# Five modulation slices summed along the rows by VectorE, and a norm turned by plain transposes, in a two-layer trunk kernel

## The chip, the cores and the metric

One core of a Trainium2 chip runs the whole kernel. Time is device microseconds, from the start of the program to its end; the median of 3 runs counts. The engines are named PE (TensorE), DVE (VectorE), ACT (ScalarE), POOL (GpSimd) and SP (SyncE, which here only issues loads).

## The reference

256 tokens of 1024 values pass two layers. A layer is a token mixer and a channel mixer; each stands behind an RMS norm, and a vector c modulates the norm's result and the residual:

```python
c_act = jax.nn.silu(c)
for layer in range(DEPTH):
    mod = c_act @ ada_w[layer] + ada_b[layer]
    sh_m, sc_m, gt_m, sh_f, sc_f, gt_f = [m[:, None, :] for m in jnp.split(mod, 6, axis=-1)]
    h = modulate(rms_norm(x, norm_mix_g[layer]), sh_m, sc_m)      # h * (1 + sc) + sh
    x = x + gt_m * hybrid_mixer(h, ...)
    h = modulate(rms_norm(x, norm_ffn_g[layer]), sh_f, sc_f)
    f = swiglu(h, ...) if layer % 2 == 0 else moe_swiglu(h, ...)
    x = x + gt_f * f
return rms_norm(x, final_g)
```

The mixer is a matrix product to 3088 columns, a gated recurrence and chunked linear attention, and an output projection. Layer 0's channel mixer is a dense SwiGLU (1024 to 2816), layer 1's picks 2 of 8 experts of that size per token. Everything is float32. What matters here is `mod`: for each layer six slices of 1024 values, each a product of one row of 1024 with a 1024 x 1024 matrix (4 MB of weights a slice, 48 MB in all).

## The kernel before, in words

**Weights.** Every weight comes from device memory in units of 128 x 2048 values (1 MB). `load` (L131 to 134) takes one of six buffers `raw` and issues the load on SP, whose queue runs in order; a buffer is free once all who read its last content are done. For most products `split` (L137 to 147) makes of 128 x 1024 weights a rounded part `whi` (ACT, L145) and the rest `wlo` (DVE, L146), in five buffers each; a product is then three matmuls, high x high, high x low and low x high (`mm3`, L155 to 159, or `stationary_pair`, L406 to 408, where the weights are the stationary operand).

**Modulation.** `ada` (L237 to 303) makes one slice in four steps, one unit of weights each, and a last step that finishes it. It has two ways. On PE (`on_dve` false): per unit four matmuls (eight records in the trace), whose stationary operand is silu(c) spread over 32 columns, add up into a bank `pb` (L261). On DVE: per unit two multiply-adds of 128 x 1024 into `acc` (L266; the first is a TENSOR_SCALAR, L264), and at the end ones-matmuls (L286) add `acc` over the partitions. For shifts and scales both ways end alike: ACT copies the bank to a `row` (L289), PE turns it by four transposes (L226) so that the values lie along partitions, and DVE adds the bias (L297, L299) and, for a scale, makes (1 + sc) * g (L301). A gate ends as a row on all partitions (L271 to 279). `put` queues slices, and `fill(n)` lets the next n steps be written at that place (L306 to 331). Which way a slice goes stands in the table `ON`: on PE sh_m, sc_m, gt_m, sh_f of layer 0 and sh_m, sc_m, gt_f of layer 1; on DVE sc_f and gt_f of layer 0 and gt_m, sh_f, sc_f of layer 1.

**Norm.** `residual` (L411 to 443) ends a layer's half: for each half of the tokens t and half of the columns c DVE multiplies the product by the gate (`y`, L440) and adds it to the stream `xs` (L441); then `block(t, c)` squares on ACT (L338). After c = 1, `rms` makes 1/rms per token (DVE L344, POOL L345), DVE scales the identity by it (`dg`, 128 x 128, L360), and PE multiplies the tokens by that diagonal (L364, eight products a half), which scales and turns them in one go. When both halves are there, ACT applies shift and scale (`h`, L377), and DVE makes of it `wide_hi` and `wide_lo` (L380, L381) for the next products. `hold` (L384) puts the first splits behind parts of that. Layer 1's last norm (`block` of the router) goes another way and isn't touched.

**Order.** The program is written in the order of the driver (L1295 to 1320): the first norm, mixer 0, dense layer (its first four fill steps, `AT_DENSE`, stand ahead of its first product), mixer 1, experts. A scheduler then sets each engine's own order from a time line that it estimates when the program is built; on the chip each engine runs its queue strictly in that order, and waits at an instruction whose operands aren't there.

Of the kernel before, what the change touches and what calls it, by code (L numbers as in the profile page):

```python
# [61 lines left out]
def trunk(  # L62
# [174 lines left out]
    def ada(layer, kind, on_dve=True, bank=pb):  # L237

        n = ("sh_m", "sc_m", "gt_m", "sh_f", "sc_f", "gt_f").index(kind)
# [11 lines left out]
        if not on_dve:  # L251
            ps = bank()
        for j in range(4):
            w = load(ada_w[layer, n, j])
# [25 lines left out]
        else:  # L280
            r = P
            if on_dve:
                r = 64
                ps = pm()
                for h in range(2):
                    pe.matmul(ps[32 * h:32 * h + 32, :], ones[:, 0:32], acc[:, h * 512:(h + 1) * 512],  # L286
                              start=True, stop=True)
# [1109 lines left out]
```

## Time and profile before

| what | value |
|---|---|
| median of 3 runs | 1167.55 us (1165.86 to 1170.02) |
| the profiled execution | 1168.7 us, its span 1166.9 us |
| granted PE clock, mean | 0.979 |
| PE busy | 1107.4 us (95%) |
| DVE busy | 627.4 us (54%) |
| ACT busy | 518.3 us (44%) |
| DMA | 395.69 MB, mean 339 GB/s |

The span is first to last instruction of one profiled execution; its own time is a little longer, and it lies 1.15 us above the median. The stages in it: first norm to about 37 us, mixer 0 to about 149, norm and dense layer to about 356, norm and mixer 1 to about 467, router and experts to the end. A granted clock of 1.00 is 2.4 GHz, 0.50 is 1.2 GHz. A busy PE counts matmuls whose ends are modelled, so 95% doesn't say that PE runs at its peak.

### The profile page before, as it was taken

To read this page: it belongs to the slowest core of one execution; us is meant where nothing else is said; L and a number is where in the kernel's file an instruction comes from. 1 tells how busy PE (TensorE), PEld (TensorE's weight loads), DVE (VectorE), ACT (ScalarE), POOL (GpSimd) and SP (SyncE) were. 2 spreads that over 40 slices of the span, in tenths; PEclk is the share of its full clock that TensorE was granted. 3 is DMA by queue.
4 is the path that set the end of the run, shared out by engine and by line. 5 is a ranking of instruction groups with operands and counts; after the bars stand their busy time and mean duration, and the time that the engine had idled before them with its cause. 6 is when DMAs were issued, how large, how long until landed. Compare 5 with 4: busy or idle time off the path is not lost.

```text
span 1166.9 us, 15801 instructions
## 1 busy us (share of the span) xinstructions
PE 1107.4 (95%) x6125; PEld 742.8 (64%) x6125; DVE 627.4 (54%) x818; ACT 518.3 (44%) x724; POOL 30.5 (3%) x69
## 2 busy tenths in 40 slices
PE   4899999999999999899999999999999999998993
PEld 2578779999777888686465445554455544655540
DVE  2668556757776765797135443353343633345442
ACT  2764444444437744786234333542342333434331
POOL 2000000000001000300000000000000000000000
PEclk9899999999999999899999999999999999998996
DMA  9977486858886447495999999999999999999994
GB/s 361 410 288 291 145 324 249 310 201 306 334 332 229 147 143 288 181 359 189 418 420 419 420 419 420 419 420 420 388 406 419 420 419 419 419 419 403 398 420 172
DMA packets 57182, 395.69 MB, mean 339 GB/s; under 512 B 8294, under 2 KB 8710, under 8 KB 9356
## 3 DMA queue, kind: packets, MB, share of 16 engines
q1 hardware_dynamic: 54272, 393.24, 84.2%
q10 hardware_dynamic: 2828, 1.37, 0.4%
q8 instruction: 50, 0.82, 0.3%
q14 instruction: 32, 0.26, 0.1%
HBM read 393.53 MB, written 1.05 MB: 338 GB/s over the span
## 4 chain that ended last, share of the span: by engine, by line
PE 88%; DMA 4%; ACT 3%; DVE 2%; POOL 1%; issue 1%; ACTq 0%; POOLq 0%; DVEq 0%; SPq 0%
PE pa L1050 17%; PE pa L158 8%; PE pa L157 8%; PE pa L159 8%; PE po L1099 7%; PE pa L406 6%; PE pa L407 6%; PE pa L408 6%; PE pb L158 4%; PE pb L159 4%; PE pb L157 4%; PE pm L226 2%; PE pb L261 2%; PE pm L973 2%; DMA bdx<-in_wx_dram 2%; ACT whi L145 2%
## 5 line engine op out<-in xcount | busy, mean ns | idle before, releaser
L146 DVE TENSOR_TENSOR wlo<-raw,whi 128x1024 fp32r<-128x1024 f32 x318 | 378.6, 1222 | 205.1 <-ACT whi L145 204.4
L145 ACT ACTIVATE whi<-raw 128x1024 fp32r<-128x1024 f32 x318 | 324.5, 1057 | 214.7 <-PE pa L407 90.2
L1050 PE MATMUL pa<-raw,x_n 128*64 128x512 f32 (+3 forms) x960 | 205.0, 562 | 0.0
L406 PE MATMUL pa<-wide_hi,whi 128*128 128x256 f32 x544 | 154.3, 284 | 0.2 <-DVE wide_hi L380 0.2
L407 PE MATMUL pa<-wide_lo,whi 128*128 128x256 f32 x544 | 153.5, 282 | 0.2 <-DVE wide_lo L381 0.2
L408 PE MATMUL pa<-wide_hi,wlo 128*128 128x256 f32 x544 | 153.5, 282 | 0.0
L1050 PEld LDWEIGHTS pa<-raw,x_n 128*64 128x64 f32 (+1 forms) x960 | 63.0, 131 | 106.7 <-issue 101.3
L158 PE MATMUL pa<-wlo,x_hi 128*128 128x512 f32 (+1 forms) x288 | 113.3, 394 | 3.7 <-DVE wlo L146 3.7
L157 PE MATMUL pa<-whi,x_hi 128*128 128x512 f32 (+1 forms) x288 | 110.7, 389 | 0.9 <-ACT whi L145 0.3
L159 PE MATMUL pa<-whi,x_lo 128*128 128x512 f32 (+1 forms) x288 | 109.9, 382 | 0.1
L406 PEld LDWEIGHTS pa<-wide_hi,whi 128*128 128x128 f32 x544 | 102.3, 188 | 6.4 <-issue 4.0
L407 PEld LDWEIGHTS pa<-wide_lo,whi 128*128 128x128 f32 x544 | 102.5, 189 | 1.6 <-issue 1.1
L408 PEld LDWEIGHTS pa<-wide_hi,wlo 128*128 128x128 f32 x544 | 102.5, 188 | 0.3 <-issue 0.3
L1099 PE MATMUL po<-raw,big 128*64 128x512 f32 (+1 forms) x440 | 93.4, 616 | 6.3 <-DMA raw<-in_m_dram 6.3
L1053 ACT ACTIVATE s<-pa 128x512 f32<-128x512 f32 (+1 forms) x30 | 16.9, 562 | 163.4 <-PE pa L1050 163.4
L158 PE MATMUL pb<-wlo,a_hi 128*128 128x512 f32 x176 | 71.6, 408 | 2.0 <-DVE wlo L146 2.0
L158 PEld LDWEIGHTS pa<-wlo,x_hi 128*128 128x128 f32 x288 | 55.3, 192 | 26.5 <-DVE wlo L146 6.7
L159 PE MATMUL pb<-whi,a_lo 128*128 128x512 f32 x176 | 69.8, 398 | 0.0
L157 PEld LDWEIGHTS pa<-whi,x_hi 128*128 128x128 f32 x288 | 55.3, 192 | 21.8 <-issue 7.7
L157 PE MATMUL pb<-whi,a_hi 128*128 128x512 f32 x176 | 60.8, 403 | 2.0 <-ACT whi L145 2.0
L1099 PEld LDWEIGHTS po<-raw,big 128*64 128x64 f32 (+1 forms) x440 | 25.4, 132 | 57.8 <-issue 49.8
L159 PEld LDWEIGHTS pa<-whi,x_lo 128*128 128x128 f32 x288 | 55.5, 193 | 10.0 <-DVE x_lo L986 0.8
(323 smaller groups left out, 1242.4 us busy)
## 6 DMA issues: line engine op xcount, KB each, us to landing
raw<-in_m_dram SPq DMA_DIRECT2D x263, 1024.0 KB, 10.6
raw<-in_ada_w_dram SPq DMA_DIRECT2D x48, 1024.0 KB, 7.3
raw<-in_f_dram SPq DMA_DIRECT2D x33, 1024.0 KB, 6.0
raw<-in_win_dram SPq DMA_DIRECT2D x20, 1024.0 KB, 6.3
raw<-in_wout_dram SPq DMA_DIRECT2D x8, 1024.0 KB, 6.1
xs<-in_x_dram SPq DMA_DIRECT2D x1, 1024.0 KB
big<-in_m_dram SPq DMA_DIRECT2D x1, 1024.0 KB
out_dram<-big SPq DMA_DIRECT2D x2, 512.0 KB, 3.2
```

The lines of the kernel that those rows point to most:

```text
L145: act.activation(hi[:, :n], src, AF.Copy)
L146: dve.tensor_tensor(lo[:, :n], src, hi[:, :n].bitcast(F32), op=ALU.subtract)
L157: pe.matmul(ps, l_hi, r_hi, start=first, stop=False)
L158: pe.matmul(ps, l_hi, r_lo, start=False, stop=False)
L159: return pe.matmul(ps, l_lo, r_hi, start=False, stop=last)
L226: return pe.transpose(o, i, ident[:i.shape[0], :i.shape[0]])
L261: pe.matmul(ps[o:o + 32, :], cact[:, k, :], wi[:, h * 512:(h + 1) * 512], start=(j == 0), stop=(j == 3))
L406: pe.matmul(pv[:, b, :], wh, h_hi[:, k, :], start=(k == 0), stop=False)
L407: pe.matmul(pv[:, b, :], wh, h_lo[:, k, :], start=False, stop=False)
L408: pe.matmul(pv[:, b, :], wl, h_hi[:, k, :], start=False, stop=(k == KD - 1))
L1050: pe.matmul(ps[r:r + m, :n], x_n[:, k, :], w[:, kk * n:(kk + 1) * n], start=(k < js), stop=(k >= KD - js))
L1099: pe.matmul(acc[r:r + m, :], aa["a_n"][:, k, :], w[:, i * 1024 + c * 512:i * 1024 + (c + 1) * 512], start=(k < js), stop=(k >= KF - js))
```

## The change

Five slices (layer 0's sc_f; layer 1's sh_m, sc_m, sh_f, sc_f) are made in a third way. Their weights lie transposed in memory: a partition holds an output value's 1024 weights. DVE multiplies them by a row silu(c) that lies on all partitions (`crow`, loaded at the start by a broadcast of 0.5 MB and passed through Silu on ACT), and one instruction's accumulator output gives the finished sum of 128 output values (`accum_out`); two such sums a unit, eight a slice, then DVE adds the bias and for a scale multiplies by g. PE and ACT have no part in it. The two gates that DVE summed stay as they were; all others stay on PE.

In the norm `dg` and the product by it go. DVE scales the tokens themselves (`tn`, 128 x 512, two a half, two buffers), and PE turns them by plain transposes, eight a half. In the first norm of all, the first split is held behind the last instruction of sc_m's modulation.

```diff
+KINDS = ("sh_m", "sc_m", "gt_m", "sh_f", "sc_f", "gt_f")
+
+SUMMED = ((0, "sc_f"), (1, "sh_m"), (1, "sc_m"), (1, "sh_f"), (1, "sc_f"))
...
+    crow = const([P, D], F32, "crow", pre)
+    act.dma_start(crow[:], c_row.to_broadcast([P, D]))
+    act.activation(crow[:], crow[:], AF.Silu)
+
+    def ada_summed(layer, kind):
+
+        n = KINDS.index(kind)
+        m = cst.tile([P, KD], F32, tag=f"{kind}{layer}", name=f"{kind}{layer}")
+        for j in range(4):
+            w = load(ada_w[layer, n, j])
+            for i in range(2):
+                b = 2 * j + i
+                acc = pre.tile([P, D], F32, tag="acc", name=nm("acc"))
+                dve.scalar_tensor_tensor(acc[:], w[:, i * D:(i + 1) * D], 1.0, crow[:], op0=ALU.mult, op1=ALU.mult,
+                                         accum_out=m[:, b:b + 1])
+            yield
+        dve.tensor_tensor(m[:], m[:], col("ab", 48 * layer + 8 * n, KD), op=ALU.add)
+        if kind[:2] == "sc":
+            dve.scalar_tensor_tensor(m[:], m[:], 1.0, col("nmg" if kind == "sc_m" else "nfg", 8 * layer, 8),
+                                     op0=ALU.add, op1=ALU.mult)
+        mod[kind, layer] = m
+        yield
+
+    def ada(layer, kind):
+        if (layer, kind) in SUMMED:
+            return ada_summed(layer, kind)
+        return ada_across(layer, kind, (layer, kind) in ((0, "gt_f"), (1, "gt_m")))
...
             rs = rms(t)
-            dg = pre.tile([P, P], F32, tag=f"dg{t}", name=nm("dg"))
-            dve.tensor_scalar(dg[:], ident[:], rs[:], 32.0, op0=ALU.mult, op1=ALU.mult)
             if t == 0:
                 turned.extend(b() for b in ((pa,) * 4 if alone else BANKS))
-            for k in range(KD):
-                pe.matmul(turned[k // 2][:, (k % 2) * SEQ + t * P:(k % 2) * SEQ + (t + 1) * P],
-                          xs[:, t, k * P:(k + 1) * P], dg[:], start=True, stop=True)
+            for j in range(2):
+                tn = pre.tile([P, 4, P], F32, tag="tn", name=nm("tn"), bufs=2)
+                dve.tensor_scalar(tn[:], xs[:, t, j * 512:(j + 1) * 512], rs[:], 32.0, op0=ALU.mult, op1=ALU.mult)
+                for i in range(4):
+                    k = 4 * j + i
+                    transpose(turned[k // 2][:, (k % 2) * SEQ + t * P:(k % 2) * SEQ + (t + 1) * P], tn[:, i, :])
...
-            hold((n0,), *((n, *m) for n, m in zip(ns, marks)))
+            hold((n0, *modded) if alone else (n0,), *((n, *m) for n, m in zip(ns, marks)))
```

The scheduler's order changes with it at two places. The first is DVE at the end of layer 0's output projection, up to the norm ahead of the dense layer. Before (`y` and `xs` of the second half of the tokens, `rs`, `dg`; the three `wlo` belong to the dense layer):

```order
L360 TENSOR_SCALAR dg_1258<-ident,rs_1255 128x128
L441 TENSOR_TENSOR xs<-xs,y_1284 128x512
L146 TENSOR_TENSOR wlo_1382<-raw_1375,whi_1381 128x1024
L440 TENSOR_TENSOR y_1302<-pa_1131,gate_m 128x512
L146 TENSOR_TENSOR wlo_1456<-raw_1435,whi_1455 128x1024
L441 TENSOR_TENSOR xs<-xs,y_1302 128x512
L146 TENSOR_TENSOR wlo_1460<-raw_1435,whi_1459 128x1024
L344 TENSOR_SCALAR rs_1307<-ss_1287 128x1
L360 TENSOR_SCALAR dg_1310<-ident,rs_1307 128x128
```

In the change the same place, from the last `y` on, where L254 is the new sum (just ahead stand the `y` before it, a `wlo`, a sum, the first `rs` and an `xs`):

```order
L464 TENSOR_TENSOR y_1308<-pa_1135,gate_m 128x512
L149 TENSOR_TENSOR wlo_1453<-raw_1442,whi_1452 128x1024
L149 TENSOR_TENSOR wlo_1457<-raw_1442,whi_1456 128x1024
L149 TENSOR_TENSOR wlo_1516<-raw_1513,whi_1515 128x1024
L386 TENSOR_SCALAR tn_1266<-xs,rs_1259 128x512
L386 TENSOR_SCALAR tn_1272<-xs,rs_1259 128x512
L465 TENSOR_TENSOR xs<-xs,y_1308 128x512
L254 SCALAR_TENSOR_TENSOR acc_1706,sc_m_1445<-raw_1704,crow 128x1024
L367 TENSOR_SCALAR rs_1313<-ss_1293 128x1
L254 SCALAR_TENSOR_TENSOR acc_1708,sc_m_1445<-raw_1704,crow 128x1024
L386 TENSOR_SCALAR tn_1316<-xs,rs_1313 128x512
L386 TENSOR_SCALAR tn_1322<-xs,rs_1313 128x512
```

Eight sums of sh_m and two of sc_m stand between the earlier `wlo`, four more of sc_m between the first `y` and the last `tn`; on PE the five fill steps of this gap are gone, and only the sixteen transposes are left there.

The second place is PE at the norm ahead of layer 1's mixer, from the last product of the dense layer. Before (L261 are the units of gt_f, whose last one follows later, L364 the products by `dg`, `gg` the columns of the recurrence's gate):

```order
L159 MATMUL pa_2818<-whi_3197,a_lo 128x512
L261 MATMUL pb_3553<-raw_3554,cact 32x512 x4
L261 MATMUL pb_3553<-raw_3621,cact 32x512 x4
L364 MATMUL pm_3241<-dg_3239,xs 128x128 x2
L364 MATMUL pm_3242<-dg_3239,xs 128x128 x2
L364 MATMUL pa_3243<-dg_3239,xs 128x128 x2
L364 MATMUL pa_3244<-dg_3239,xs 128x128 x2
L364 MATMUL pm_3241<-dg_3291,xs 128x128 x2
L364 MATMUL pm_3242<-dg_3291,xs 128x128 x2
L364 MATMUL pa_3243<-dg_3291,xs 128x128 x2
L364 MATMUL pa_3244<-dg_3291,xs 128x128 x2
L261 MATMUL pb_3553<-raw_3627,cact 32x512 x4
```

In the change (L293 are the units of gt_f, L229 the transposes):

```order
L162 MATMUL pa_2806<-whi_3190,a_lo 128x512
L293 MATMUL pb_3539<-raw_3540,cact 32x512 x4
L293 MATMUL pb_3539<-raw_3607,cact 32x512 x4
L229 MATMUL pm_3232<-ident,tn_3236 128x128 x2
L229 MATMUL pm_3233<-ident,tn_3236 128x128 x2
L229 MATMUL pa_3234<-ident,tn_3242 128x128 x2
L229 MATMUL pa_3235<-ident,tn_3242 128x128 x2
L293 MATMUL pb_3539<-raw_3613,cact 32x512 x4
L229 MATMUL pm_3232<-ident,tn_3286 128x128 x2
L229 MATMUL pm_3233<-ident,tn_3286 128x128 x2
L229 MATMUL pa_3234<-ident,tn_3292 128x128 x2
L229 MATMUL pa_3235<-ident,tn_3292 128x128 x2
```

The third unit of gt_f has moved ahead of the second half's transposes, and the ones-matmuls (L286) of sc_f are gone.

## Rows read from the trace of the kernel before

**Rows 1.** The page, part 4: shares of the chain that ended last, by engine.

```profile
PE 88%; DMA 4%; ACT 3%; DVE 2%; POOL 1%; issue 1%; ACTq 0%; POOLq 0%; DVEq 0%; SPq 0%
```

**Rows 2.** Windows by stage: us, busy per engine, PEclk, DMA share, GB/s.

```profile
0.00:60.00 60.00, 40.56 (x278) 25.69 (x279) 28.40 (x77) 28.39 (x46) 5.90 (x23) 0.91 0.97 379
...
160.00:240.00 80.00, 80.00 (x671) 77.08 (x670) 52.01 (x57) 37.38 (x45) 0.00 (x0) 1.00 0.79 295
...
540.00:1166.00 626.00, 592.57 (x2819) 315.68 (x2817) 264.52 (x308) 222.61 (x320) 2.09 (x2) 0.98 0.97 400
```

**Rows 3.** Chain of waits, 128 to 226: start, us, what.

```profile
137.10 0.98 PE pm L286 x4
...
143.40 0.39 PE pm L226 x4
...
165.16 0.99 PE pb L261 x8
...
174.31 0.44 PE pm L226 x4
```

**Rows 4.** Time line 140 to 160, PE and DVE: start, us, engine, operation [idle before].

```profile
142.97 0.69 DVE L440 TENSOR_TENSOR y<-pb,gate_m 128x512 f32<-128x512 f32 x1 [0.45 <-PE pb L159]
...
148.81 2.76 PE L261 MATMUL pb<-raw,cact 128*32 128x512 f32 x18
...
151.39 1.22 DVE L146 TENSOR_TENSOR wlo<-raw,whi 128x1024 fp32r<-128x1024 f32 x1
...
152.53 0.21 DVE L344 TENSOR_SCALAR rs<-ss 128x1 f32<-128x1 f32 x1
...
156.19 1.16 PE L364 MATMUL pm<-dg,xs 128*128 128x128 f32 x8
...
157.99 0.43 DVE L380 CAST wide_hi<-h 128x512 fp32r<-128x512 f32 x1 [4.31 <-ACT h L377]
...
158.48 0.50 PE L406 MATMUL pa<-wide_hi,whi 128*128 128x256 f32 x2 [0.23 <-DVE wide_hi L380]
```

**Rows 5.** Groups by line and form, 0 to 560: busy us, mean ns.

```profile
L146 DVE TENSOR_TENSOR wlo<-raw,whi 128x1024 fp32r<-128x1024 f32 x164 | 198.6, 1222 | 82.1 <-ACT whi L145 81.8 <-PE pb L261 0.2
...
L266 DVE SCALAR_TENSOR_TENSOR acc<-raw,cs,acc 128x1024 f32<-128x1024 f32 x37 | 47.4, 1281 | 11.1 <-DMA raw<-in_ada_w_dram 7.6 <-DMA acc<-in_ada_b_dram 3.1
...
L338 ACT ACTIVATION_READ_ACCUMULATOR junk<-xs 128x1 f32 x16 | 3.0, 186 | 0.0
...
L264 DVE TENSOR_SCALAR acc<-raw,cs 128x1024 f32<-128x1024 f32 x3 | 2.2, 749 | 1.5 <-PE pm L286 1.5
```

**Rows 6.** Windows of 4 us, 472 to 488: columns as in rows 2.

```profile
472.00:476.00 4.00, 1.16 (x13) 1.01 (x13) 3.35 (x17) 3.82 (x5) 0.00 (x0) 0.71 1.01 428
...
480.00:484.00 4.00, 4.00 (x15) 3.52 (x15) 2.05 (x4) 4.00 (x7) 3.31 (x9) 0.51 0.32 131
484.00:488.00 4.00, 4.00 (x23) 3.23 (x22) 1.34 (x3) 1.78 (x4) 2.07 (x8) 1.00 0.00 0
```

**Rows 7.** Time line 352 to 368, SP, PE and DVE.

```profile
356.24 0.81 SPq L134 DMA_DIRECT2D raw<-in_ada_w_dram  x2
...
359.68 1.16 PE L364 MATMUL pm<-dg,xs 128*128 128x128 f32 x8 [0.22 <-DVE dg L360]
...
361.48 0.43 DVE L380 CAST wide_hi<-h 128x512 fp32r<-128x512 f32 x1 [1.11 <-ACT h L377]
...
361.66 1.07 PE L261 MATMUL pb<-raw,cact 128*32 128x512 f32 x8
...
365.97 0.69 DVE L381 TENSOR_TENSOR wide_lo<-h,wide_hi 128x512 fp32r<-128x512 f32 x1
...
367.79 0.28 PE L159 MATMUL pa<-wide_hi,gg 128*16 128x256 f32 x1
```

**Rows 8.** Tile raw, 94 to 170: its loads.

```profile
DMA to landing us min/median/max: 4.8/7.6/12.5
```

**Rows 9.** Chain of waits, 0 to 50.

```profile
26.08 8.81 DMA raw<-in_ada_w_dram
```

More of the change, by code (lines that the diff above doesn't have):

```diff
@@ L67, in trunk @@
     ada_w: bass.AP,
+    c_row: bass.AP,
     ada_b: bass.AP,
@@ L235, in trunk, with ada_across @@
         dve.tensor_tensor(pick[:, h:h + 1], ident[:, 32 * h:32 * h + 1], ident[:, 32 * h + 64:32 * h + 65], op=ALU.add)
-    def ada(layer, kind, on_dve=True, bank=pb):
-        n = ("sh_m", "sc_m", "gt_m", "sh_f", "sc_f", "gt_f").index(kind)
+    crow = const([P, D], F32, "crow", pre)
[22 more added lines that the diff above has]
+        return ada_across(layer, kind, (layer, kind) in ((0, "gt_f"), (1, "gt_m")))
+    def ada_across(layer, kind, on_dve):
+        n = KINDS.index(kind)
         is_gate = kind[:2] == "gt"
@@ L262, in ada @@
                                   start=(j == 0), stop=(j == 3))
-                elif k == 0 and not is_gate:
-                    dve.tensor_scalar(acc[:], wi, cs[:, 0:1], None, op0=ALU.mult)
                 else:
@@ L280, in ada @@
         else:
[L281 to L287, printed above, removed]
             row = wk.tile([P, 512], F32, tag="s", name=nm("row"))
-            act.activation(row[:r], ps[:r], AF.Copy)
+            act.activation(row[:], ps[:], AF.Copy)
             tp = pm()
             for b in range(4):
-                transpose(tp[:, b * P:b * P + r], row[:r, b * P:(b + 1) * P])
+                transpose(tp[:, b * P:(b + 1) * P], row[:, b * P:(b + 1) * P])
             tv = tp[:].rearrange("p (b i h c) -> p c i h b", i=2, h=2, c=32)[:, 0]
@@ L297, in ada @@
             dve.tensor_tensor(mv, tv[:, 0], bv, op=ALU.add)
-            if not on_dve:
-                dve.tensor_tensor(mv, tv[:, 1], mv, op=ALU.add)
+            last = dve.tensor_tensor(mv, tv[:, 1], mv, op=ALU.add)
             if kind[:2] == "sc":
-                dve.scalar_tensor_tensor(m[:], m[:], 1.0, col("nmg" if kind == "sc_m" else "nfg", 8 * layer, 8),
-                                         op0=ALU.add, op1=ALU.mult)
+                last = dve.scalar_tensor_tensor(m[:], m[:], 1.0, col("nmg" if kind == "sc_m" else "nfg", 8 * layer, 8),
+                                                op0=ALU.add, op1=ALU.mult)
             mod[kind, layer] = m
+            modded[:] = [last]
         yield
@@ L1298, in trunk @@
     hs = {}
-    put(ada(0, "sh_m", *ON[7]), ada(0, "sc_m", *ON[7]))
+    put(ada(0, "sh_m"), ada(0, "sc_m"))
     fill(X_AT)
@@ L1307, in trunk @@
     modulate()
-    put(ada(0, "gt_m", *ON[0]), ada(0, "sh_f", *ON[1]), ada(0, "sc_f", *ON[2]))
+    put(ada(0, "gt_m"), ada(0, "sh_f"), ada(0, "sc_f"))
     mixer(0, FILLS[0], *hs["m", 0], lambda: None, lambda: fresh("f", 0)[0])
-    put(ada(1, "sh_m", *ON[8]), ada(1, "sc_m", *ON[8]), ada(0, "gt_f", *ON[3]), ada(1, "gt_m", *ON[4]), ada(1, "sh_f", *ON[5]),
-        ada(1, "sc_f", *ON[9]))
+    put(ada(1, "sh_m"), ada(1, "sc_m"), ada(0, "gt_f"), ada(1, "gt_m"), ada(1, "sh_f"),
+        ada(1, "sc_f"))
     dense(0, 1, *hs["f", 0], lambda: fresh("m", 1)[0])
-    put(ada(1, "gt_f", *ON[6]))
+    put(ada(1, "gt_f"))
     mixer(1, FILLS[1], *hs["m", 1], router_set, router_block)
@@ L1356, in moe_units, with ada_units @@
         return np.concatenate([half_units(w[:, :2560]), k_units(w[:, 2560:], 256)])
+    def ada_units(w):
+        w = w.reshape(DEPTH, D, 6, D).transpose(0, 2, 1, 3)
+        u = f(w.reshape(DEPTH, 6, 4, 2, P, D).transpose(0, 1, 2, 4, 3, 5).reshape(DEPTH, 6, 4, P, 2 * D))
+        for layer, kind in SUMMED:
+            i = KINDS.index(kind)
+            t = w[layer, i].T.reshape(4, 2, P, D).transpose(0, 2, 1, 3)
+            u[layer, i] = t.reshape(4, P, 2 * D)
+        return u
     return {
@@ L1360, in _layouts @@
         "cols": f(cols),
-        "ada_w": f(a["ada_w"].reshape(DEPTH, 4, 2, P, 6, D).transpose(0, 4, 1, 3, 2, 5).reshape(DEPTH, 6, 4, P, 2 * D)),
+        "ada_w": ada_units(a["ada_w"]),
+        "c_row": f(a["c"].reshape(1, D)),
         "ada_b": f(a["ada_b"]),
```

5 lines of the change are left out of this document (2 added, 3 removed).

## The prediction

> **What bounds the kernel now.** I read the shares of the chain first: TensorE (PE) carries 88% of the chain that ended last [rows 1]. Then the busy time by stage [rows 2]: in the first 60 us the DMA share is 0.97, in the dense layer (160 to 240) PE is busy 80.00 of 80 us at full clock, and from 540 on the DMA share is 0.97 again at 400 GB/s over 626 us. So every microsecond that the front (to about 540) ends earlier or later is carried 1:1 to the end, because the stage behind it streams its weights at a rate that the change doesn't touch. Third, the time line around the two norms that the change rewrites, since PE is the engine to ask about: is it idle there, and which engine's last step lets it go on?
>
> **The slices that leave PE.** Two slices of layer 1 (sh_m, sc_m) go from PE to VectorE (DVE), and three that DVE summed already lose their tail on PE. In the dense layer's chain three steps of eight matmuls at 0.99 us each go, two groups of four transposes at 0.44, and one pair of ones-matmul and transposes, 0.98 + 0.39 [rows 3] (the pair shown is that of layer 0's sc_f, at 137 to 144; layer 1's sh_f has the same two durations at 320 to 327; one of the three steps and one of the two groups stand there). 3 x 0.99 + 2 x 0.44 + 1.37 = **5.2 us less**, all of it on the path since PE is busy 80 of 80 us there [rows 2]. The other five steps of these two slices stand in the norm gap, from 148.81 on, where PE waits for the norm anyway [rows 4]; the pair at 137 to 144 lets PE end layer 0's output projection 1.37 us earlier. Both belong to the gap, next.
>
> **The gap of the norm ahead of the dense layer.** Before: PE is done with the projection when its fills begin at 148.81, turns the second half of the tokens from 156.19, and the first matmul on the normed tokens (L406) starts at 158.48 [rows 4]. DVE isn't late in it: it waits 4.31 us for ScalarE's h ahead of its wide_hi at 157.99. After: DVE's queue runs strictly in the order written, and that order now holds sums among the residual's y and xs. The second y can't start before its matmul, 142.97 - 1.37 = 141.6. From it to the tn that PE waits for (the second half's first) stand y x3, xs x4, wlo x4, sums x4, tn x2 and rs x2. A y or xs is 0.69 [rows 4], a wlo 1.22 [rows 5], an rs 0.21 [rows 4]. A **tn** (128 x 512 times two scalars) is not in the trace: half of the 128 x 1024 TENSOR_SCALAR's 749 ns [rows 5] gives 0.37 below, wide_hi's 0.43 for the same size above [rows 4]; I take 0.43. A **sum with accumulate** isn't either: below it is the same instruction without one, 1.28; above it I add ScalarE's read of its accumulator, 0.19 [rows 5]; I take 1.28. So 7 x 0.69 + 4 x 1.22 + 4 x 1.28 + 2 x 0.43 + 2 x 0.21 = 16.2 us, to 157.8, and the tn itself to 158.2. Before, 2.29 us lay between the second half's first PE instruction and L406 [rows 4]; four transposes take 0.44 [rows 3] where the four matmuls took about 0.66 (1.16 for eight), which leaves 2.1. L406 then starts at 160.4 instead of 158.48: **+2.0**. Ends: these durations overlap by some 0.08 each (the rs at 152.53 begins 1.14 behind a wlo of 1.22 [rows 4]), 20 of them give -1.6; the accumulator reads of these four and of the ten sums ahead give up to 14 x 0.19 = +2.7. So 0.4 to 4.7.
>
> The Trainium skill, page "VectorE: DVE Perf Modes", section "Two Vector instructions with no wait between them", says that a Vector operation that also writes out its accumulator is two instructions, the operation and a read of the accumulator. No row of VectorE here shows it. It names no duration, so the upper end above stays the one from ScalarE's row.
>
> **The clock behind that gap.** PE, without fills, has only sixteen transposes to do between 147.4 and 160.4. What a wait does to its clock is in the trace once, ahead of the experts [rows 6]: in 472 to 476 PE is busy 1.16 of 4 us and the granted clock 0.71, then two stretches of 4 us at half (0.51 in 480 to 484, and the one ahead of it alike: 1.2 GHz) with PE at work, and 1.00 (2.4 GHz) again from 484. So about 8 us of work at half speed follow: 3.8 lost as upper bound; none below (if the transposes keep the clock). PE is idle here longer than there, so I take the fall as the likelier; the transposes from 158.2 already use up 2.2 of the 8 us, so (7.6 - 2.2) / 2 = **+2.7**.
>
> The Trainium skill, page "TensorE: Matmul & The Clock Gate", section "Part 4: PE-mode transpose", says that the clock's full rate doesn't engage for transpose-mode work, as it doesn't count as busy in the same way. That speaks against this change, which puts transposes where matmuls stood; by it the 3.8 would be the value, 1.1 more in the sum. No row here shows transposes alone.
>
> **The gap of layer 1's norm.** DVE's part is short here: tn x4 instead of two dg. But the order on PE is new: the third unit of gt_f now stands ahead of the second half's transposes, where it stood behind. Its load goes out at 356.24 [rows 7]. Loads took 4.8 us at the least, 7.6 in the median and 12.5 at the most [rows 8] (the row is of 94 to 170, the nearest stretch); this one had landed by 361.66, when its step ran [rows 7]. So it lands between 361.0 and 361.66; I take 361.3. With a step of 0.99 [rows 3] the transposes start at 362.3 instead of 359.68 [rows 7]. wide_hi followed by 1.80; with transposes shorter by 0.2 that is 363.9 instead of 361.48, and the chain of wide_hi and wide_lo, 5.2 us long (361.48 to 366.66 [rows 7]), ends at 369.1. PE's gate matmuls, eight sets of 0.35, ended at 368.1 [rows 7], four sets behind that chain; now two sets are left behind it: 369.8 at the latest, +1.7. Nothing is lost if the chain closes up, as ScalarE and DVE have time while PE waits. I take **+1.0**, between 0 and 1.7. For the clock a wait of 3 us comes with it, shorter than the one in [rows 6]: 0 to 3.8, a third of it, **+1.2**.
>
> **The start.** The row of silu(c) for all partitions is one more 0.524 MB in a stretch that moves data all the time (share 0.97, 379 GB/s [rows 2]): 1.4 us. The chain there is a load of 8.81 us from 26.08 on, which PE's gt_m step waits for until 35.0 [rows 9]. **+1.4**, 0 if that load goes ahead of it, 2.8 at most if its packets share badly. Silu over 128 x 1024 and its table loads lie on ScalarE ahead of 35, under the same load; the later first split (held behind sc_m) too, for PE has its gt_m step to wait for; without that cover it would be a whi and a wlo, 2.3 us.
>
> **Sum.** 1.4 + 2.0 + 2.7 - 5.2 + 1.0 + 1.2 = **+3.1** on the profiled execution of 1168.7 us, that is 1171.8. The median is 1.15 below that execution: **1170.6 us**.
>
> **Rivals.**
> *The clock holds (faster).* For it: around both norms the clock stayed at 1.00, and fills as well as transposes are work. Against it: [rows 6]. Then 2.7 and 1.2 go, and with DVE's overlap (-1.6) the sum is 3.1 - 5.5 = -2.4; if the row's load also lands unnoticed (-1.4), -3.8: 1163.7. Decided by PEclk just behind L406.
> *A sum waits for its weights (slower).* The third unit of sc_m is only requested once the sum that frees its buffer is done. By the durations above that is at 148.1, and DVE comes to the sums on it at 155.0, 6.9 later. With the 7.6 of the median landing it is 0.7 late, with 12.5 it is 5.6 [rows 8]; y, tn and thus PE's transposes stand behind it on DVE. In the middle +3.1, with both clock terms whole (+3.7): 3.1 + 6.8 = +9.9, 1177.4. For it: a queue in order, and 16 us of work on it. Against: the DMA has little else to do at that time. It decides from a landing above 6.9 us.
> *PE gains nothing in the dense layer.* If its weights (share 0.79 in 160 to 240) or wlo come too late once the fills are gone, 5.2 is given back to a wait: 1175.8. Against: PE waited for neither in 80 us.
>
> **How the numbers follow.** The forecast with its own spread: 0.45; the clock holds: 0.22; a late load: 0.23; no gain in the dense layer: 0.10. A change of 0.3%, 3.5 us, is about what a measurement of this kernel can tell from none: below 1164.0 is faster, above 1171.1 slower. The forecast lies just inside, so its 0.45 falls 0.30 within and 0.15 slower (the ends of the unknown costs are wider upward); the first rival falls 0.22 around the lower edge, most of it beyond since the parts of the gain come together, 0.16, and 0.06 within; the others 0.29 slower and 0.04 within. With some weight (0.05) for a gap that closes altogether (DVE's sums under PE's work: L406 up to 5 us earlier), taken from these: faster 0.21, within 0.38, slower 0.41. The range 1162.5 to 1177.5 takes in the first rival with a little beyond it and the second's middle value.
>
> **What would show it.** L406's first start behind the last matmul of the projection: 13 us now right, 9.6 (as before) or less wrong. PEclk 0.5 for some microseconds behind it. PE without idle time in the dense layer, and that layer shorter by 5.2. DVE's sums in the residual without a wait for a DMA, each near 1.28. Layer 1's transposes of the second half behind a unit of gt_f. The forecast is wrong if DVE has free time ahead of the second half's tn, or if a sum takes 1.5 us or more.

## The result, and the profile after

The changed kernel takes **1174.48 us** (median, 1171.71 to 1175.91) beside 1168.3 us of the kernel before in the same series: 1.0051 times as long, 95% interval 1.0041 to 1.006. So it is slower, by about 6 us. The predicted 1170.6 us was a plus of 3.1; the time lies inside the range, and the forecast had put 0.41 on slower and 0.38 on no difference. The prediction counted from a median of 1167.55 us.

The page of the changed kernel, part 4, the chain that ended last by engine (it answers to [rows 1]), and windows by stage (to [rows 2]): us, busy time of PE, PEld, DVE, ACT and POOL, granted PE clock, DMA share, GB/s.

```profile
PE 79%; DMA 7%; DVE 5%; ACT 4%; issue 3%; POOL 1%; POOLq 0%; ACTq 0%; SPq 0%; DVEq 0%
```

```profile
160.00:240.00 80.00, 75.95 (x605) 74.92 (x605) 54.17 (x65) 36.34 (x46) 2.42 (x2) 0.93 0.64 236
174.00:355.00 181.00, 181.00 (x1266) 168.19 (x1266) 128.94 (x144) 80.19 (x88) 2.88 (x3) 1.00 0.74 279
0.00:60.00 60.00, 36.85 (x227) 21.27 (x228) 25.31 (x72) 29.41 (x47) 5.92 (x23) 0.91 0.95 369
```

PE has lost 9 points of the chain to DMA, DVE, ACT and issue. In the dense layer it still works without a pause (181.00 of 181 us); what is new lies around it. The two profiled executions (spans 1166.9 and 1173.0 us) are compared at six marks on PE, the start of the named matmul (`wg` is a small weight of the recurrence's gate; its product is the first behind the gate columns `gg`):

| stretch | before | after | difference | predicted |
|---|---|---|---|---|
| start to mixer 0's first matmul by `wg` | 43.02 | 45.85 | +2.8 | +1.4 |
| to the projection's last matmul | 105.46 | 105.20 | -0.3 | -1.4 |
| to the dense layer's first (the gap) | 10.00 | 16.25 | +6.3 | +3.4 |
| dense layer, to its last | 196.74 | 193.03 | -3.7 | -2.5 |
| to mixer 1's first by `wg` (second gap) | 13.40 | 16.85 | +3.5 | +2.2 |
| mixer 1, to its projection's last | 98.48 | 97.20 | -1.3 | 0 |
| router, experts, end | 699.80 | 698.62 | -1.2 | 0 |
| sum | 1166.9 | 1173.0 | +6.1 | +3.1 |

(The predicted column spreads the prediction's terms over the stretches: the pair of 1.37 that leaves the projection comes back in the gap, and the clock's 2.7 stands with the dense layer.)

The gap on DVE, time line of the changed kernel from 142 (start, us, engine, line, operation, idle before and who ended it). L254 is a sum, L464 `y`, L386 `tn`:

```profile
142.40 1.23 DVE L254 SCALAR_TENSOR_TENSOR acc<-raw,crow 128x1024 f32<-128x1024 f32 x1 [1.77 <-DMA raw<-in_ada_w_dram]
143.55 0.08 DVE L254 DVE_READ_ACCUMULATOR acc<-raw,crow 128x1 f32 x1
143.55 1.22 DVE L149 TENSOR_TENSOR wlo<-raw,whi 128x1024 fp32r<-128x1024 f32 x1
...
146.85 1.29 DVE L464 TENSOR_TENSOR y<-pb,gate_m 128x512 f32<-128x512 f32 x2 [0.94 <-PE pb L162]
...
149.95 1.23 DVE L254 SCALAR_TENSOR_TENSOR acc<-raw,crow 128x1024 f32<-128x1024 f32 x1 [0.61 <-DMA raw<-in_ada_w_dram]
...
155.31 3.48 DVE L149 TENSOR_TENSOR wlo<-raw,whi 128x1024 fp32r<-128x1024 f32 x3
158.71 0.88 DVE L386 TENSOR_SCALAR tn<-xs,rs 128x512 f32<-128x512 f32 x2
...
161.56 1.23 DVE L254 SCALAR_TENSOR_TENSOR acc<-raw,crow 128x1024 f32<-128x1024 f32 x1 [1.38 <-DMA raw<-in_ada_w_dram]
...
164.50 0.88 DVE L386 TENSOR_SCALAR tn<-xs,rs 128x512 f32<-128x512 f32 x2 [0.43 <-POOL rs L368]
```

The same stretch on PE (L229 are the transposes, L430 the dense layer's first matmul), and its granted clock in windows of 4 us, columns as above:

```profile
151.05 0.39 PE L162 MATMUL pa<-whi,ee 128*128 128x512 f32 x1
159.34 1.09 PE L229 MATMUL pm<-ident,tn 128*128 128x128 f32 x4 [7.89 <-DVE tn L386]
...
165.04 1.12 PE L229 MATMUL pm<-ident,tn 128*128 128x128 f32 x4 [3.76 <-DVE tn L386]
...
167.30 0.79 PE L430 MATMUL pa<-wide_hi,whi 128*128 128x256 f32 x2 [0.29 <-DVE wide_hi L404]
```

```profile
150.00:154.00 4.00, 1.44 (x7) 0.84 (x5) 4.00 (x7) 3.97 (x6) 0.00 (x0) 0.98 0.15 29
154.00:158.00 4.00, 0.00 (x0) 0.00 (x0) 4.00 (x8) 0.72 (x2) 0.92 (x1) 0.50 0.83 326
158.00:162.00 4.00, 1.94 (x8) 1.57 (x8) 2.62 (x5) 0.72 (x2) 0.00 (x0) 0.50 1.00 367
162.00:166.00 4.00, 0.96 (x5) 0.96 (x6) 2.94 (x7) 0.23 (x1) 1.46 (x1) 0.50 0.47 117
166.00:170.00 4.00, 3.71 (x16) 3.08 (x15) 2.97 (x6) 3.57 (x8) 0.00 (x0) 0.50 0.53 223
170.00:174.00 4.00, 4.00 (x32) 4.00 (x32) 1.33 (x3) 0.17 (x1) 0.00 (x0) 0.88 0.01 4
```

PE waits 7.89 and 3.76 us, both times for `tn`, and `tn` stands behind sums and splits on DVE; three of these sums wait for their weights. The clock has fallen to 1.2 GHz in 154 to 158, while PE does nothing at all, and is back at 2.4 GHz only at about 171, four microseconds into the dense layer.

The second gap on PE, where [rows 7] show it before: L293 is the third unit of gt_f.

```profile
362.51 0.66 PE L229 MATMUL pm<-ident,tn 128*128 128x128 f32 x4
363.01 0.60 PE L229 MATMUL pa<-ident,tn 128*128 128x128 f32 x4
367.04 1.94 PE L293 MATMUL pb<-raw,cact 128*32 128x512 f32 x8 [3.43 <-DMA raw<-in_ada_w_dram]
368.90 0.90 PE L229 MATMUL pm<-ident,tn 128*128 128x128 f32 x3
```

The second half's transposes wait behind a unit whose weights land 3.43 us after PE was free.

### The profile page after: what moved, and what is told of

Its sections match the earlier page's. It is cut to its first block, busy times and chain, and to the rows that moved or that the text cites. A ratio compares the mean times of both kernels' runs of the same rounds, so it can differ in the third digit from the quotient of the medians.

```text
span 1173.0 us, 15574 instructions
## 1 busy us (share of the span) xinstructions
PE 1092.7 (93%) x5981; PEld 735.6 (63%) x5981; DVE 647.5 (55%) x878; ACT 519.2 (44%) x722; POOL 32.8 (3%) x69
## 4 chain that ended last, share of the span: by engine, by line
PE 79%; DMA 7%; DVE 5%; ACT 4%; issue 3%; POOL 1%; POOLq 0%; ACTq 0%; SPq 0%; DVEq 0%
PE pa L1074 16%; PE pa L161 7%; PE pa L160 7%; PE po L1123 7%; PE pa L162 7%; PE pa L430 5%; PE pa L431 5%; PE pa L432 5%; PE pb L161 4%; PE pb L162 4%; PE pb L160 3%; DMA raw<-in_m_dram 3%; DVE wlo L149 2%; PE pm L229 2%; DMA raw<-in_ada_w_dram 2%
## 5 line engine op out<-in xcount | busy, mean ns | idle before, releaser
L430 PE MATMUL pa<-wide_hi,whi 128*128 128x256 f32 x544 | 155.2, 287 | 0.3 <-DVE wide_hi L404 0.3
L430 PEld LDWEIGHTS pa<-wide_hi,whi 128*128 128x128 f32 x544 | 104.1, 192 | 5.0 <-issue 2.3
L431 PEld LDWEIGHTS pa<-wide_lo,whi 128*128 128x128 f32 x544 | 103.7, 191 | 0.5 <-issue 0.2
L432 PEld LDWEIGHTS pa<-wide_hi,wlo 128*128 128x128 f32 x544 | 103.8, 191 | 0.3 <-issue 0.3
L1077 ACT ACTIVATE s<-pa 128x512 f32<-128x512 f32 (+1 forms) x30 | 16.9, 562 | 157.1 <-PE pa L1074 157.1
```

The source lines that it names most:

```text
L430: pe.matmul(pv[:, b, :], wh, h_hi[:, k, :], start=(k == 0), stop=False)
L431: pe.matmul(pv[:, b, :], wh, h_lo[:, k, :], start=False, stop=False)
L432: pe.matmul(pv[:, b, :], wl, h_hi[:, k, :], start=False, stop=(k == KD - 1))
L1077: act.activation(a[:, :n], ps[:, :n], AF.Copy)
```

## The experiments

All runs in one table: median and ratio to the kernel before in the same series (there were four, in which it took 1168.3 to 1168.95 us), and from the one profile of each the marks of the table above (start to mixer 0's `wg`, end of the projection, length of the gap, of the dense layer and of the second gap). The last column is the span from the first one-hot matmul behind the router to the end, a stretch that no edit touches.

| kernel | median us | ratio [95%] | start | proj. end | gap | dense | 2nd gap | experts |
|---|---|---|---|---|---|---|---|---|
| before | 1168.3 | 1 | 43.0 | 148.5 | 10.0 | 196.7 | 13.4 | 690.6 |
| after | 1174.5 | 1.0051 [1.0041, 1.0060] | 45.9 | 151.1 | 16.3 | 193.0 | 16.9 | 689.5 |
| e1 | 1170.9 | 1.0027 [1.0017, 1.0037] | 42.5 | 149.5 | 8.8 | 196.8 | 16.9 | 688.5 |
| e2 | 1169.0 | 1.0004 [0.9995, 1.0013] | 46.2 | 149.9 | 15.4 | 190.7 | 13.8 | 689.1 |
| e3 | 1171.5 | 1.0032 [1.0018, 1.0046] | 45.9 | 151.2 | 9.3 | 195.1 | 17.0 | 689.6 |
| e4 | 1172.9 | 1.0039 [1.0025, 1.0052] | 42.8 | 148.1 | 16.6 | 193.3 | 16.8 | 691.3 |
| e5 | 1170.8 | 1.0022 [1.0009, 1.0034] | 44.6 | 148.3 | 9.9 | 191.8 | 17.3 | 694.3 |
| e6 | 1170.9 | 1.0021 [1.0004, 1.0039] | 45.8 | 149.5 | 15.7 | 193.2 | 14.0 | 690.0 |
| e7 | 1165.7 | 0.9972 [0.9962, 0.9983] | 42.6 | 146.4 | 13.7 | 190.7 | 13.3 | 690.5 |
| e8 | 1159.5 | 0.9920 [0.9907, 0.9934] | 42.1 | 145.8 | 11.7 | 190.7 | 13.7 | 688.3 |
| e9 | 1167.9 | 0.9994 [0.9982, 1.0006] | 42.3 | 147.8 | 8.8 | 196.8 | 15.1 | 691.1 |
| e10 | 1162.2 | 0.9954 [0.9936, 0.9972] | 42.7 | 147.9 | 7.7 | 192.3 | 14.1 | 690.3 |
| e11 | 1164.3 | 0.9969 [0.9958, 0.9979] | 42.2 | 145.9 | 9.2 | 195.1 | 14.3 | 690.7 |

### The two halves of the change, apart

**e1, the norm alone** (all modulation as before):

```diff
-            dg = pre.tile([P, P], F32, tag=f"dg{t}", name=nm("dg"))
-            dve.tensor_scalar(dg[:], ident[:], rs[:], 32.0, op0=ALU.mult, op1=ALU.mult)
...
+                tn = pre.tile([P, 4, P], F32, tag="tn", name=nm("tn"), bufs=2)
```

> The kernel before with the norm's part of the change alone (tn and plain transposes), the slices made as before. Theory (the sums and the row's load cost most; the norm costs only by the order on PE in layer 1's gap, where the third unit of gt_f stands ahead of the second half's transposes): start as before, the gap ahead of the dense layer within 1 us of the 9.7 of before, since the fills still lie in it, layer 1's gap 2 to 3.5 longer: about +2.5 us, ratio 1.001 to 1.003. Rival A (the norm isn't part of the loss): 0, ratio within 0.001 of 1. Rival B (transposes in place of matmuls cost the clock wherever they stand): PEclk 0.5 behind both norms and +5 us or more.

1170.88 us, slower by 2.3, as expected. The first gap is 1.2 us shorter, the second 3.5 longer: as in the changed kernel a unit of gt_f has come ahead of the second half's transposes, and PE waits 3.61 us for its load. In the first gap the fills are still there, between the transposes. Time line of e1 on PE, and its windows:

```profile
149.81 2.77 PE L261 MATMUL pb<-raw,cact 128*32 128x512 f32 x20
152.51 0.66 PE L226 MATMUL pm<-ident,tn 128*128 128x128 f32 x4
```

```profile
150.00:154.00 4.00, 4.00 (x35) 1.52 (x30) 3.81 (x5) 1.48 (x4) 0.00 (x0) 1.00 0.64 223
154.00:158.00 4.00, 3.33 (x28) 1.33 (x20) 1.33 (x4) 1.91 (x5) 0.55 (x1) 1.00 1.01 428
```

Sixteen transposes ran at 2.4 GHz, four in 0.66 us; behind an idle PE four took 1.09.

**e2, the sums alone** (the norm by `dg` again):

```diff
+            dve.tensor_scalar(dg[:], ident[:], rs[:], 32.0, op0=ALU.mult, op1=ALU.mult)
...
-                dve.tensor_scalar(tn[:], xs[:, t, j * 512:(j + 1) * 512], rs[:], 32.0, op0=ALU.mult, op1=ALU.mult)
```

> The changed kernel with the old norm (dg and the product by it). Theory: start 4 late and the gap ahead of the dense layer 15 to 16 us as in the change, with a clock of 0.5 behind it although matmuls stand where the transposes stood; layer 1's gap as before since its third unit of gt_f is back behind the second half: about +3 to +4 us against before, 2 to 3 less than the change. Rival A (the norm isn't part of the loss): +6 as the change. Rival B (the transposes cost the clock): the clock stays at 1.00 behind the gap, and the loss is under 2 us.

1168.95 us, no difference from before, where +3 to +4 was expected. The gap is there (15.4 us) and the late start too, as the theory had them; the dense layer is 6.1 us shorter and the second gap about as before (13.8). Against the changed kernel it gains 2.4 us in the dense layer, which the expectation didn't have, and 1.5 in mixer 0 (103.7 us from `wg` to the projection's end, 105.2 there), on which the last section says what is known. Its windows in the gap:

```profile
150.00:154.00 4.00, 0.28 (x2) 0.00 (x0) 4.00 (x7) 3.52 (x5) 0.92 (x1) 0.84 0.46 139
154.00:158.00 4.00, 0.73 (x3) 0.76 (x4) 3.72 (x5) 0.18 (x1) 0.00 (x0) 0.50 1.01 418
158.00:162.00 4.00, 3.20 (x16) 2.90 (x15) 2.79 (x6) 0.54 (x2) 1.46 (x1) 0.50 0.61 229
162.00:166.00 4.00, 4.00 (x19) 4.00 (x20) 1.79 (x4) 2.52 (x6) 0.00 (x0) 0.50 0.73 262
```

There is no transpose of tokens in this kernel, and the clock falls all the same, behind an idle time of 6.99 us. Its sixteen products by `dg`, which the trace shows as 32 matmuls, use up the slow time (eight take 1.91 to 2.08 us) and nearly nothing of it is left for the dense layer.

**e3, three sums** (layer 1's sh_m and sc_m back on PE):

```diff
-SUMMED = ((0, "sc_f"), (1, "sh_m"), (1, "sc_m"), (1, "sh_f"), (1, "sc_f"))
+SUMMED = ((0, "sc_f"), (1, "sh_f"), (1, "sc_f"))
```

> The changed kernel with layer 1's sh_m and sc_m back on PE (three slices summed instead of five). Theory: the sums in the residual's queue were the loss in the gap ahead of the dense layer, so that gap is back at 9 to 10 us at full clock; start still 4 late; dense layer 1.4 shorter than before instead of 5.2; layer 1's gap long as in the change: +2 to +4 against before. Rival (the gap is long because of the norm's own DVE work and transposes, not the sums): the gap stays above 12 us and the total at +5 or more.

1171.46 us, as expected. With these two slices back on PE, and with them the fills in the gap, it is 9.3 us long and the clock there 1.00; so the gap and the slow clock come from moving sh_m and sc_m. The dense layer is 1.6 us shorter than before (the tail of sh_f that left PE); the late start and the second gap remain.

### The start

**e4, the row of silu(c) loaded later.** ACT's queue issues its load only behind the first splits, at some 50 us:

```diff
-    act.dma_start(crow[:], c_row.to_broadcast([P, D]))
...
+        with tc.issue_after(last_split[0].ins):
+            act.dma_start(crow[:], c_row.to_broadcast([P, D]))
```

> The changed kernel with the load of the row silu(c) and its Silu held behind a split of the mixer's first weights (about 50 us) instead of ahead of the small loads on ScalarE's queue. Theory (the row's load delays the small loads behind it on that queue, ScalarE waits for them before it squares the second half of the tokens, and PE, in order, stands at that half's transposes): the first norm is back at the times of before, the first gate matmul at 37 instead of 39.2, and 3 to 4 us come back: 1170.5 to 1171.5. Rival (only its 0.5 MB count, in a stretch that is bound by loads anyway): 1.4 at most comes back, none if the stretch from 50 on is bound too: 1173 to 1174.5.

The start is 3.0 us earlier than in the changed kernel, and that is still there at the projection's end (148.1 against 151.1). Of this the median shows 1.6 (1172.93), so the expected 3 to 4 us didn't come in the total, which is at the rival's edge; in the profiles the experts' stretch took 1.8 back. At the start itself 3.0 is over the rival's 1.4. What the row did is on ACT's queue. Time line of the changed kernel:

```profile
1.30 0.49 ACTq L242 DMA_DIRECT2D crow<-in_c_row_dram  x1
2.50 1.41 ACTq L482 DMA_DIRECT2D bda<-in_wa_dram  x2
...
16.00 0.63 ACT L361 ACTIVATE junk<-xs 128x512 f32<-128x512 f32 x1 [2.98 <-DMA bda<-in_wa_dram]
...
18.93 1.11 PE L229 MATMUL pa<-ident,tn 128*128 128x128 f32 x4 [3.46 <-DVE tn L386]
19.98 1.94 PE L293 MATMUL pb<-raw,cact 128*32 128x512 f32 x8
```

and of e4:

```profile
13.49 0.63 ACT L367 ACTIVATE junk<-xs 128x512 f32<-128x512 f32 x1 [0.99 <-DMA bda<-in_wa_dram]
```

The small loads behind the row come later, ACT waits 2.98 us for one of them in place of 0.99, its squares, `tn` and PE's transposes follow, and the units of modulation that stand behind these transposes free their buffers later. The loads then run dry for a while: in 24 to 28 the DMA share is 0.56 in the changed kernel and 1.02 in e4 (changed kernel first):

```profile
24.00:28.00 4.00, 3.21 (x28) 0.96 (x24) 0.54 (x3) 0.80 (x2) 0.00 (x0) 1.00 0.56 167
```

```profile
24.00:28.00 4.00, 1.64 (x16) 0.16 (x8) 0.29 (x1) 0.31 (x1) 0.00 (x0) 0.97 1.02 375
```

e4 takes both out of this stretch, the row's bytes and its place in the queue; how the 3.0 us divide between the two was not tried.

### The sums ahead of the norm

**e5, the sums of layer 1's sc_m held** behind the norm's last `wide_lo` on DVE:

```diff
+                    if (layer, kind) == (1, "sc_m"):
+                        order.enter_context(tc.issue_after(scaled[0].ins))
+                    dve.scalar_tensor_tensor(acc[:], w[:, i * D:(i + 1) * D], 1.0, crow[:], op0=ALU.mult, op1=ALU.mult,
...
```

> The changed kernel with the sums of layer 1's sc_m held behind the last wide_lo of the norm ahead of the dense layer, so that none of them stands between that norm's y and tn. Theory (the gap is long because four sums, 1.15 each, and their waits for weights, 3.8 together, stand in DVE's queue ahead of the tn): the gap from the projection's last matmul to the first matmul of the dense layer falls from 16.3 to 8 to 10 us, and 6 to 8 us come back there; some of it may go to the dense layer's start, whose weights now share the six buffers with units that wait: 1167 to 1170 in all. Rival (DVE's work as a whole is the limit, wherever the sums stand): the gap shortens, but PE waits for wlo or weights in the dense layer instead, and less than 3 us come back.

1170.78 us, just over the expected 1167 to 1170. The gap closes to 9.9 us, about that of the kernel before, as expected. Mixer 0's end is 2.8 us earlier as well, but that isn't the edit: up to it PE has the same instructions in the same order as in the changed kernel, and 1.3 of the 2.8 lie at the start, 1.5 in mixer 0. At the router the profiled execution is 9.1 us ahead of the changed kernel; at the end it is 4.3 ahead (1168.7 against 1173.0), and the medians differ by 3.7. The expert stage took the rest: 694.3 us, with 402 GB/s in 700 to 850 where the kernel before had 414. No instruction of it is changed, and I have no cause for it.

### The unit of gt_f in the second gap

**e6, the third unit of gt_f held on PE behind the last transpose:**

```diff
+                            if (layer, kind) == (1, "gt_f") and j == 2:
+                                order.enter_context(tc.issue_after(tnd[0].ins))
+                            pe.matmul(ps[o:o + 32, :], cact[:, k, :], wi[:, h * 512:(h + 1) * 512],
...
```

> The changed kernel with the third unit of layer 1's gt_f held behind the last transpose of layer 1's norm on PE, as it stood before. Theory (PE stands 3.4 us at that unit's load with the transposes behind it, and pays for it with the clock): that gap falls from 16.9 to 13.5 to 14 us, 3 us come back: 1171 to 1172. Rival (the wait for the load only moves behind the transposes, to the gate matmuls): under 1 us comes back.

1170.89 us, 3.6 under the changed kernel. The second gap is 14.0 us: 2.8 of the 3.5 that it had grown are the place of this one unit. The first gap is nearly unchanged (15.7, a sum again waits 1.52 us for its weights). The profiles lie 4.1 us apart; 1.5 of these are in mixer 0 (103.7 against 105.2), where the two kernels run the same instructions in the same order.

**e9, e1 with the same unit held** (the norm alone, its order mended):

> No sums; the norm by plain transposes, and the third unit of layer 1's gate weights held behind the transposes on TensorE. Theory (the later layer-1 start of the norm-alone kernel is the order of that one unit, not the transposes): gap ahead of the dense layer about 8.8 us and its stretch 196.7 as in the norm-alone kernel, gap between the layers 13.4 to 14.0 in place of 16.9, so some 3 us under the norm-alone kernel: about 1167 us, ratio 0.998 to 1.000. Rival (the norm itself makes the gap longer): gap between the layers 16 to 17 again and 1170 to 1171 us, ratio about 1.0025.

1167.93 us, ratio 0.9994: equal to before. The second gap is 15.1 us, between the two expectations: the unit runs at half speed (1.83 us, in the kernel before 1.07), and so do the ones-matmuls behind it (1.92 against 1.03). In this order the norm by transposes costs nothing and brings nothing that can be measured in the total.

### Put together

**e7, e2 with e4's and e5's edits** (the norm by `dg`), and **e8, the changed kernel with e4's, e5's and e6's edits:**

> The five sums of the change with the old norm (dg), the row's load held to about 50 us, and sc_m's sums held behind the norm. If the parts of the loss add up (start 3, gap 7, layer 1's gap 3), what is left is the gain on PE in the dense layer, 5.2, and the pair of 1.4: 5 to 7 us faster than before, 1161 to 1164. Rival (the held sums only move the loss into the dense layer, or the expert stage takes back what the front gains): within 2 us of before.

> The same with the new norm (tn, plain transposes) and the third unit of gt_f held behind its transposes. Theory (transposes or products by dg are of one price once the order around them is the same): within 1.5 us of the kernel with the old norm, 1161 to 1164. Rival (tn and transposes cost by themselves, through DVE's four scalings and a lower clock): 2 us or more slower than it.

e7 takes 1165.72 us, 3.2 less than before: under the 5 to 7 of its theory, over the 2 of its rival. e8 takes **1159.46 us** (1158.38 to 1160.82), ratio 0.992 [0.9907, 0.9934]: 9.5 us less than the kernel before and 15 less than the changed one, and the best here. It was to lie within 1.5 of e7 or be slower, and neither came. Of the 6.3 between the two 2.0 lie in the gap; 1.4 lie in mixer 1 and 2.2 in the experts' stretch, where neither edit works. Beside the kernel before it is alike: 3.6 of the 10.3 us between the profiles lie in mixer 1 and behind it. e8 in the gap, PE and DVE:

```profile
153.52 1.09 PE L230 MATMUL pm<-ident,tn 128*128 128x128 f32 x4 [7.28 <-DVE tn L398]
...
157.51 0.65 PE L443 MATMUL pa<-wide_hi,whi 128*128 128x256 f32 x2 [0.29 <-DVE wide_hi L416]
```

```profile
146.63 1.22 DVE L150 TENSOR_TENSOR wlo<-raw,whi 128x1024 fp32r<-128x1024 f32 x1
...
148.36 1.22 DVE L150 TENSOR_TENSOR wlo<-raw,whi 128x1024 fp32r<-128x1024 f32 x1
...
150.10 1.22 DVE L150 TENSOR_TENSOR wlo<-raw,whi 128x1024 fp32r<-128x1024 f32 x1
...
152.90 0.87 DVE L398 TENSOR_SCALAR tn<-xs,rs 128x512 f32<-128x512 f32 x2
```

PE is still idle for 7.28 us, and three splits stand ahead of `tn`.

**e10, e8 with more of the dense layer's splits held behind the norm:**

```diff
-HOLD_N = {0: (1, 0, 0, 0, 3), "f": (0,), 1: (2, 0, 0, 0, 2)}
+HOLD_N = {0: (1, 0, 0, 0, 3), "f": (2, 0, 0, 0, 3), 1: (2, 0, 0, 0, 2)}
```

> The changed kernel with crow late, the sums of (1,sc_m) held, the third gate unit behind the transposes, and three more of the dense layer's weight splits (wlo) held behind the last wide_lo, so that three times 1.14 us less stand ahead of rs and tn on VectorE. Theory (the order on VectorE still sets what is left of the gap): gap 8.3 us in place of 11.67, dense stretch unchanged at 190.7, about 1156 us, ratio 0.989. Rival (the splits are missed at the start of the dense layer, or the last projection's copies set the gap): gap 11 to 12 or a dense stretch longer by as much, 1159 to 1161 us, ratio 0.992.

The gap closes to 7.7 us, as the theory had it and a little more, PE waits 3.47 us in place of 7.28; yet the kernel is 2.7 us slower than e8 (1162.17), and the expected 1156 is missed by 6. The end of the projection is 2.1 us later, the dense layer 1.6 longer, mixer 1 1.4, the experts 2.0. The dense layer's part is the clock: it falls behind the shorter wait too, and with the layer starting sooner (155.6, in e8 157.5) more of the slow time falls into it (e10 first, then e8):

```profile
158.00:162.00 4.00, 4.00 (x29) 4.00 (x28) 3.97 (x7) 3.34 (x5) 0.00 (x0) 0.78 0.00 0
```

```profile
158.00:162.00 4.00, 3.92 (x33) 3.76 (x32) 3.79 (x8) 2.04 (x4) 0.00 (x0) 1.00 0.00 0
```

On the projection's and mixer 1's part the last section says what is known; the experts' part has no reason that I know of.

**e11, e8 with three sums only:**

> Only three slices by sums (those of sh_m and sc_m of layer 1 back on TensorE), crow late, the third gate unit behind the transposes. Theory (the sums of sh_m and sc_m are worth what TensorE saves in the dense layer, about 4 us, once they are out of the way of the norm): gap about 9 us, dense stretch 195.1, gap between the layers 14, about 1163 to 1165 us, ratio 0.995 to 0.997, 4 to 5 us over the kernel with all five. Rival (these two slices bring nothing, all the gain is in the start and the norm): 1159 to 1161 us, ratio 0.992.

1164.32 us, 4.9 over e8, as the theory said (4 to 5). In the dense layer the two slices are worth 195.1 - 190.7 = 4.4; e11's gap is 2.5 shorter, with the fills back in it, and its expert stage 2.4 longer, so that the total agrees in part by chance. That the slices bring nothing is out by the dense layer alone.

## Why the prediction was right, and where its terms were off

**What bounds the kernel.** The front's time did reach the end, but not 1:1 within a microsecond: the experts' stretch, which no edit touches, took 688.3 to 694.3 us over the thirteen profiles. "Carried 1:1" needs some 3 us either way on a single profile.

**Slices off PE: -5.2, measured -6.1.** e2, e7 and e8, whose clock is full almost from the layer's first matmul on, need 190.7 us where the kernel before needs 196.7. e3 gives the tail alone 1.6 (predicted 1.37), which leaves 4.4 for the steps and transposes of sh_m and sc_m (3.85). PE waits for nothing in it, so the third rival is out: the changed kernel has PE at 181.00 of 181 us there.

**The gap: +2.0, measured +4.9** (6.25 less the 1.37 that the projection no longer has). The mechanism, sums and splits ahead of `tn` on DVE and PE idle behind it, is right, and e5 shows it by taking the sums away, e10 for the splits. The 2.9 that were missing: the second `y` starts 3.6 us ahead of the projection's last matmul (about 147.45 against 151.05), where I had it 5.5 ahead (142.97 against 148.48), 1.9; from there to the second half's `tn` 17.0 us in place of 16.2, 0.8; from `tn` to the dense layer 2.8 in place of 2.6. The 0.8 hide errors that offset each other. The terms given add up to 16.1, not 16.2, and the overlap that I counted at the lower end only (-1.6) is real: a sum takes 1.15 from start to start where I took 1.28. Against that two of the four sums counted wait 0.61 and 1.38 us for weights, and `tn` waits 0.43 for the `rs` on POOL, which takes 1.46 us beside a sum (0.55 in the kernel before). The 1.38 is the second rival, the sum on sc_m's third unit that waits for its weights, come true at less than half of its middle price (3.1); one of the prediction's own signs, sums without a wait for a DMA, failed with it.

**The clock: +2.7, measured +2.3.** The changed kernel's dense layer needs 193.03 us, e8's 190.69. The Trainium skill, page "TensorE: Matmul & The Clock Gate", section "Part 4: PE-mode transpose", would have had the transposes themselves as the reason. The rows differ: the clock falls in 154 to 158 with PE at 0.00 busy; it falls in e2 with no such transposes; and it holds 1.00 in e1 with sixteen of them between fills. So the fall came with PE's idle time and not with the transposes, and the rival that the clock holds is out. Whether transposes with no other work around them would hold the clock, no run shows. The prediction says that the trace of before has such a fall once; it has another in the first norm, 0.50 in 32 to 40.

**The second gap: +2.2, measured +3.5.** The place of the unit was read rightly from the order, and e6 shows it to be 2.8 of the 3.5. The size was off since the load went out 1.46 us behind the dense layer's last matmul (361.79; before it was 1.02), and since the unit then ran at half speed, 1.94 us where I had 0.99.

**The start: +1.4, measured +2.8** at mixer 0's `wg`. This is the step that failed in kind: I counted the row's bytes and laid Silu and the row's place "under the same load". e4 gives 3.0 back, more than the 1.4 of the bytes, and the traces show the rest: with the row ahead of them on ACT's queue the small loads come late, and in 24 to 28 the weights' loads stand still for nearly half of the time. It was to be seen: the order on ACT puts the row's load ahead of the small loads that ACT's squares wait for. The size is rough: the kernels with the row in this place reach `wg` at 44.6 to 46.2 us, all others at 42.1 to 43.0.

**Mixer 0: -1.4, measured -0.3.** The pair did leave it. The 1.1 that are missing are the clock in 48 to 52, behind a wait of PE. I can't lay them on the change: e6 has the same instructions in the same order up to here and the same start, and its clock held (changed kernel first, then e6):

```profile
48.00:52.00 4.00, 4.00 (x24) 4.00 (x23) 0.49 (x2) 3.89 (x5) 0.00 (x0) 0.57 1.01 418
```

```profile
48.00:52.00 4.00, 4.00 (x36) 4.00 (x36) 0.48 (x1) 3.92 (x5) 0.00 (x0) 1.00 1.02 422
```

**Not foreseen: -2.5**, in mixer 1 (-1.3, below) and from the router to the end (-1.2, within the spread of that stretch). Without these the sum would have been +8.6, that is 1176.2, close to the upper end of the range: start, gap and second gap were all three too small, and only the dense layer's gain was too small the other way. That the total came out 3 us off and not 5 or 6 is luck.

## What to carry to other kernels

A new instruction's price is less its own time than its place: read from the order, on every queue it is put on, which waiting work it now precedes, and price that. The fills that PE did in the gap kept its clock at 1.00 (e1, e3, e11), without them it fell to 0.50; whoever moves such work away should ask first what else fills the gap, and put the moved work behind what the gap waits for: the same change cost 6 us in one order and gained 9.5 in another, though some 3.6 of the gain lie where no edit works.
